# Reordered small work in a two-layer hybrid attention trunk: first squares, rotary roots, key copies, first output chunk

## The chip, the cores and the metric

The kernel runs on one core of one Trainium2 chip. The time is the device time of one execution in microseconds (us). Three runs of the kernel before gave a median of 1243.19 us (1242.96 to 1244.62). TensorE (PE) multiplies, VectorE (DVE), ScalarE (ACT) and GpSimd (POOL) do the elementwise work, and SyncE (SP) issues almost all transfers. Each engine works through its own queue in order.

## The reference

The trunk has two layers over two groups of tokens, 512 of a prompt and 256 of a sample, with 1024 channels. Each layer does, for each group:

```python
mod = silu(c) @ w_ada + b_ada                      # shift, scale, gate
hid = rms_norm(x, norm_g) * (1 + scale) + shift
qa, ka, va, za, qb, kb, vb, zb, ga, gb = split(hid @ w_in)
oa = neighbourhood_attention(qa, ka, va, rpb)      # 8 heads of 64, on a grid
ya = (oa * silu(za)) @ w_pa
ob = gqa(rope(rms_norm(qb)), rope(rms_norm(kb)), vb)   # 8 query heads, 2 key heads
yb = (ob * silu(zb)) @ w_pb
merged = sigmoid(ga) * ya + sigmoid(gb) * yb
x = x + gate * (merged @ w_out)
```

A last rms_norm ends the trunk. All arithmetic is float32.

## The kernel before

**Products.** Every matrix product is done in three passes on operands that are split into a high and a low part: high by high, low by high, high by low. The weights come from memory in units of 128 x 1024 (`raw`). ScalarE copies a unit to its high part (`whi`, line 222), and VectorE subtracts to get the low part (`wlo`, line 228); two or three units of a layer go to GpSimd instead. The helper `mm` at line 115 records every product, so that products are told apart by the tile they write: `accp` and `accs` are chunks of 256 output channels for the prompt and the sample, `accw` and `acct` have the tokens on the partitions.

**Stages of a layer.** The value projection of the neighbourhood branch (`va`), four head pairs of queries and keys with the neighbourhood attention beside them (`sp`, `tp`, `op`), the queries (`qb`) and the keys and values (`kvb`) of the grouped branch with norms and rotary positions, the gate `za`, then four pairs of chunks `ga`, `pa` with the grouped attention beside them (`gsp` scores, `gp` probabilities, `gtp` their transposes, `go` the product with the values), `zb`, four pairs `gb`, `pb` with the vectors of the next modulation computed on VectorE beside them (`adaacc`), and the output projection `wo`, first for the prompt and then for the sample.

**What sets the order.** The kernel's text is run once to write the program, under a manual schedule, so the order of its calls is the order in each engine's queue. The unit is a step: 6 to 12 products of one chunk, written by `step(fn)`. After each step the function writes what `defer(k, fn)` put off by k steps, then one piece of `chain` (the norm and the modulation of the next layer), then pieces of the attention from `slots` at a set rate, and pieces of `side` (`adaacc`). A table `SC` holds the offsets: the scaled keys come `KF` steps after the last step of `kvb`, their transposes `KT` steps after it, the grouped attention starts `SGQ` steps after it, the query roots and transposes of the prompt `QF` and `QT` steps after the queries' third pass, and `DP` steps after the prompt's output chunks the next norm starts. `ahead` splits the next chunk's weight units at two set steps of a chunk. In the 3 pieces of `rms_chain` the sum over channels is a product with ones (`ssps`), then come Newton steps for the inverse root on VectorE (`ny`, `na`, 11 small instructions), and then a product that spreads the roots (`rb`).

**The start.** The start of the program is planned: `job` records pieces with an engine, a duration and dependencies, `load` records transfers with times, and `run_jobs` writes all in order of the planned times. Squares of the 8 tiles of `x` are taken by ScalarE (`sq`) and added up by VectorE, two of them by GpSimd. The modulation vectors of the first layer are products on TensorE (`adap`) of 32 loaded pieces (`adaraw`), which come back through `rows` (ACT) and `adat` (PE). Products on zeroes (`junk`) keep TensorE running: 18 at first and then one for each 0.45 us of planned time.

**Grouped attention's entry.** `rope_finish` takes the roots of 32, 16 or 12 sums for each token and scales the rotated tiles (`rr`). `ktr` transposes the six key tiles (`kt`), and `evac_k` copies each to two places on ScalarE (`GK`, lines 675 and 676) and writes two low parts on VectorE (lines 679 and 680). The scores of the grouped attention rotate through two buffers: a third `gsp` needs the first one's row maximum (`gss`, line 902) and exponential (line 912) done.

## Time and profile before

| | |
|---|---|
| median of 3 runs | 1243.19 us |
| profiled execution, its own time | 1244.36 us |
| its span, first to last instruction | 1242.6 us |
| mean granted TensorE clock | 0.995 |
| PE busy | 1208.7 us (97%) |
| DVE busy | 818.4 us (66%) |
| ACT busy | 580.6 us (47%) |
| POOL busy | 347.6 us (28%) |

A row of a timeline gives the start, the duration, the engine, the line, what is written from what, and in square brackets how long the engine sat idle before it and what released it. A row of the waits gives who waited for whom: the sum in us, how often, and the longest. A row of the windows gives, for each stretch of the span, its length, the busy time of PE, PEld (weight loads), DVE, ACT and POOL with the number of instructions, the granted TensorE clock, the share of the DMA engines and GB/s.

### The profile page before, as it was taken

Reading aid. Unit: us, or ns where it says so; the run is one execution under the profiler, and the core shown is the slowest. Engines: PE = TensorE matmul, PEld = TensorE weight load, DVE = VectorE, ACT = ScalarE, POOL = GpSimd, SP = SyncE. Lnnn points to the kernel's source line nnn. Section 1 sums busy time; section 2 is a strip of 40 time slices with the busy share of each in tenths; the row PEclk is TensorE's granted clock in tenths of the full one; section 3 lists DMA queues with packets and bytes.
Section 4 is the critical chain, followed back from the end, with each engine's and each line's share of the span. In section 5 each row is a group of like instructions: output and inputs, shape, how many; then the busy total and the mean of one; then the engine's idle time right before and its main releaser. Section 6 shows DMA issues by size and latency. Waiting matters only on the chain.

```text
span 1242.6 us, 19501 instructions
## 1 busy us (share of the span) xinstructions
PE 1208.7 (97%) x7282; PEld 1058.6 (85%) x7282; DVE 818.4 (66%) x1609; ACT 580.6 (47%) x1229; POOL 347.6 (28%) x383
## 2 busy tenths in 40 slices
PE   8999999989999999999989999998999999999997
PEld 5789988879898988887888998897988998888887
DVE  5757877775556558998384688777566545683435
ACT  4447755445545332333153776554555543232323
POOL 0024555342223121121131443553322212121102
PEclk9999999999999999999999999999999999999999
DMA  9343411111011234556352324112011113332334
GB/s 350 138 124 94 108 54 54 49 51 35 26 44 51 69 107 149 170 169 202 119 172 88 93 74 124 35 38 65 18 52 52 35 35 102 119 105 66 119 102 152
DMA packets 48125, 118.28 MB, mean 95 GB/s; under 512 B 5408, under 2 KB 11936, under 8 KB 48032
## 3 DMA queue, kind: packets, MB, share of 16 engines
q1 hardware_dynamic: 47888, 116.98, 30.6%
q8 instruction: 57, 0.93, 0.3%
q14 instruction: 36, 0.29, 0.1%
q10 hardware_dynamic: 144, 0.07, 0.0%
HBM read 110.74 MB, written 6.29 MB: 94 GB/s over the span
## 4 chain that ended last, share of the span: by engine, by line
PE 78%; DVE 11%; ACT 5%; issue 3%; DMA 1%; POOL 1%; SPq 0%; DVEq 0%; ACTq 0%; POOLq 0%
PE accp L115 35%; PE accs L115 17%; PE accw L115 8%; PE go L115 3%; PE gsp L115 3%; PE gtp L937 3%; PE acct L115 3%; DVE adaacc L445 3%; DVE wlo L228 2%; ACT p L775 1%; PE sp L115 1%; PE op L115 1%; ACT whi L222 1%; PE adap L115 1%; DVE ptl L704 1%
## 5 line engine op out<-in xcount | busy, mean ns | idle before, releaser
L115 PE MATMUL accp<-hh,whi 128*128 128x512 f32 x512 | 204.3, 399 | 0.0
L115 PE MATMUL accp<-hh,wlo 128*128 128x512 f32 x512 | 201.2, 393 | 2.1 <-DVE wlo L228 2.1
L115 PE MATMUL accp<-hl,whi 128*128 128x512 f32 x512 | 201.2, 393 | 0.0
L228 DVE TENSOR_TENSOR wlo<-raw,whi 128x1024 fp32r<-128x1024 f32 x119 | 159.1, 1338 | 21.1 <-ACT whi L222 20.5
L115 PE MATMUL accs<-hh,whi 128*128 128x256 f32 x512 | 146.4, 286 | 0.0
L115 PE MATMUL accs<-hh,wlo 128*128 128x256 f32 x512 | 145.0, 283 | 0.0
L115 PE MATMUL accs<-hl,whi 128*128 128x256 f32 x512 | 144.9, 283 | 0.0
L926 POOL TENSOR_TENSOR gp<-gp,gss 128x512 f32<-128x512 f32 x80 | 83.4, 1042 | 213.8 <-DVE gss L924 192.5
L222 ACT ACTIVATE whi<-raw 128x1024 fp32r<-128x1024 f32 x124 | 129.7, 1053 | 17.7 <-PE accw L115 8.2
L115 PEld LDWEIGHTS accp<-hh,wlo 128*128 128x128 f32 x512 | 96.8, 189 | 24.9 <-DVE wlo L228 3.8
L115 PEld LDWEIGHTS accp<-hl,whi 128*128 128x128 f32 x512 | 97.1, 190 | 17.5
L115 PEld LDWEIGHTS accp<-hh,whi 128*128 128x128 f32 x512 | 96.8, 189 | 17.7
L699 ACT ACTIVATE pth<-gtp 128x512 fp32r<-128x512 f32 x80 | 47.7, 597 | 111.2 <-PE go L115 90.2
L115 PEld LDWEIGHTS accs<-hh,whi 128*128 128x128 f32 x512 | 98.2, 192 | 1.0
L115 PEld LDWEIGHTS accs<-hl,whi 128*128 128x128 f32 x512 | 98.2, 192 | 1.0
L115 PEld LDWEIGHTS accs<-hh,wlo 128*128 128x128 f32 x512 | 98.0, 191 | 0.0
L1539 POOL TENSOR_TENSOR th<-th 128x512 f32<-128x512 f32 (+1 forms) x32 | 43.5, 1371 | 171.2 <-DVE th L1532 171.2
L445 DVE SCALAR_TENSOR_TENSOR adaacc<-adaraw,csil,adaacc 128x512 f32<-128x512 f32 x112 | 86.6, 829 | 3.6 <-DMA adaraw<-in_wsd 3.6
L722 POOL TENSOR_TENSOR bm<-u,masks 128x128 f32<-128x128 f32 (+2 forms) x80 | 41.3, 539 | 152.4 <-DMA u<-in_rpb 152.4
L704 DVE TENSOR_TENSOR ptl<-gtp,pth 128x512 fp32r<-128x512 f32 x80 | 54.7, 685 | 40.5 <-ACT pth L699 40.4
L115 PE MATMUL accw<-whi,hh 128*128 128x512 f32 x192 | 77.3, 403 | 0.0
L115 PE MATMUL accw<-wlo,hh 128*128 128x512 f32 x192 | 75.3, 392 | 0.0
(245 smaller groups left out, 2965.7 us busy)
## 6 DMA issues: line engine op xcount, KB each, us to landing
raw<-in_wst SPq DMA_DIRECT2D x124, 512.0 KB, 3.6
adaraw<-in_wsd SPq DMA_DIRECT2D x64, 256.0 KB, 3.1
adaraw<-in_wad SPq DMA_DIRECT2D x32, 256.0 KB, 6.0
u<-in_rpb SPq DMA_DIRECT2D x16, 354.5 KB, 4.8
u<-in_rpb SPq DMA_DIRECT2D x16, 236.5 KB, 4.4
out_y<-y SPq DMA_DIRECT2D x12, 256.0 KB, 2.5
x<-in_xT SPq DMA_DIRECT2D x8, 256.0 KB, 5.0
res<-in_xT SPq DMA_DIRECT2D x8, 256.0 KB, 3.0
```

The costliest lines, as they stand in the source:

```text
L115: T.matmul(out=out, lhsT=lhsT, rhs=rhs, start=start, stop=stop, skip_group_check=True)
L222: A.activation(out=hi, in_=r, func=AF.Copy)
L228: eng.tensor_sub(out=lo, in0=r, in1=hi.bitcast(F32))
L445: V.scalar_tensor_tensor(out=acc[n, h, g], in0=r, scalar=c, in1=acc[n, h, g], op0=ALU.mult, op1=ALU.add)
L699: A.activation(out=h, in_=t, func=AF.Copy)
L704: V.tensor_sub(out=lo, in0=t, in1=h.bitcast(F32))
L722: G.tensor_tensor(out=o.rearrange("p (c r) -> p c r", r=r), in0=u, in1=mk.rearrange("p (c r) -> p c r", r=r), op=ALU.add)
L775: A.activation(out=P[:, j, :], in_=P[:, j, :], func=AF.Exp, scale=-1.0, bias=ss[:, j:j + 1], accum_out=ss[:, 2 + j:3 + j])
L926: G.tensor_mul(out=pv_, in0=pv_, in1=ss[:, 4:4 + n].unsqueeze(2).to_broadcast([128, n, w]))
L937: T.transpose(t[:, q, 128 * j:128 * j + 128], src, ident)
L1539: G.tensor_add(out=t[:, sl], in0=t[:, sl], in1=mrg[k][:, sl])
```

## The change

**The start.** All adding of squares goes to VectorE, in order of the tiles, for tiles 0 to 6; tile 7's squares are summed by a product of their own, into the same accumulator. The products on zeroes are 30 at once, and then one for each gap of over 0.5 us that the plan leaves on TensorE up to 20 us. The planned transfers move by 0.7 us and the plan's delay between engines goes from 0.12 to 0.22 us.

**Norms.** An empty piece stands between the Newton steps and the spreading product, and `DP` is 5 in place of 6. For the sample's norm of the second layer there is one empty piece more.

**Rotary roots.** The Newton steps are written in two halves one step apart, and the scalings one step each after them. The offsets move: `QF` 5 to 4, `QT` 9 to 10, `QS` 6 to 5, `QST` 12 to 13, `KF` 7 to 5.

**Keys.** The transposes and copies are done for the prompt at step 12 (before: all at 13) and for the sample at 14, and the second key head's copies follow one step after the first's. The grouped attention starts at step 15 in place of 16.

**Weights and the first output chunk.** In chunks four tiles deep (`pa`, `pb`) the next units are split at steps 2 and 4 in place of 3 and 6, and in the sample's output chunks at 1 and 2 in place of 2 and 3. In the first output chunk the products with the last two merged tiles are put behind all others of that chunk.

```diff
-    T0=3.6,
+    T0=4.3,
-    WARM=(18, 18.0, 0.45),
+    WARM=(30, 20.0),
-    QF=5,  QT=9,  QS=6,  QST=12,  KF=7,  KT=13,  SGQ=16,  DP=6,
+    QF=4,  QT=10, QS=5,  QST=13,  KF=5,  KT=12,  SGQ=15,  DP=5,
...
     def paired(pieces):
-        return pieces[0:3] + [sum(pieces[i:i + 2], []) for i in range(3, len(pieces), 2)]
+        return pieces[0:4] + [sum(pieces[i:i + 2], []) for i in range(4, len(pieces), 2)]
...
-    def newton(x, n):
+    def newton_parts(x, n):
+
         y = smp.tile([128, n], F32, tag=f"ny{n}", name="ny", bufs=1)
         a = smp.tile([128, n], F32, tag=f"na{n}", name="na", bufs=1)
...
+        return y, [first, refine, refine, refine]
+
+    def newton(x, n):
+        y, parts = newton_parts(x, n)
+        for fn in parts:
+            fn()
         return y
...
-        return [[a_], [b_], [c_]]
+        return [[a_], [b_], [], [c_]]
...
-    def feat_chunk(name, src, nk, evac, ksteps=2, groups=(0, 1), keep=False, sep=False):
+    def feat_chunk(name, src, nk, evac, ksteps=2, groups=(0, 1), keep=False, sep=False, late=False):
...
+            kk = per * (1 + g)
+            seq = [(m, k0) for m in range(2) for k0 in range(0, nk, kk)]
+            if late:
+                seq = [p for p in seq if p[1] < nk - kk] + [p for p in seq if p[1] == nk - kk]
+            for m, k0 in seq:
...
-                        if not (keep and name[2] == 3) and cnt[0] in ((3, 6) if len(groups) == 2 else (3, 5) if groups[0] == 0 else (2, 3)):
+                        if not (keep and name[2] == 3) and cnt[0] in ((2, 4) if nk == 4 else (3, 6) if len(groups) == 2 else (3, 5) if groups[0] == 0 else (1, 2)):
                             ahead(name)
...
-        def run_jobs(lag=0.12):
+        def run_jobs(lag=0.22):
...
+            n0, until = SC["WARM"]
+            t = 1.8 + 0.3 * n0
+            for j in sorted((j for j in jobs if j["eng"] == "PE"), key=lambda j: done[j["n"]]):
+                start = done[j["n"]] - j["dur"]
+                while t + 0.5 < min(start, until):
+                    out.append((t, -1, lambda: warm(1)))
+                    t += 0.3
+                t = max(t, done[j["n"]])
+            warm(n0)
...
-        def sq_sum():
-            hcell["ps"] = ps_acc.tile([128, 4], F32, tag="acc", name="ssps")
+        def sq_sum(k, first, last):
+            if first:
+                hcell["ps"] = ps_acc.tile([128, 4], F32, tag="acc", name="ssps")
             for i in range(4):
-                mm(hcell["ps"][:, i:i + 1], sq[0, 0][:, 128 * i:128 * i + 128], ones[:, 0:1], i == 0, i == 3)
-            gfree(sq.pop((0, 0)))
+                mm(hcell["ps"][:, i:i + 1], sq[0, k][:, 128 * i:128 * i + 128], ones[:, 0:1],
+                   first and i == 0, last and i == 3)
+            gfree(sq.pop((0, k)))
...
-        jg = job("POOL", 1.2, [js[2], js[3]], lambda: sq_add(0, 3, 2, G), 1)
-        j = js[0]
-        for k, d in ((1, js[1]), (4, js[4]), (2, jg), (5, js[5]), (6, js[6]), (7, js[7])):
-            j = job("DVE", 0.75, [j, d], lambda k=k: sq_add(0, k, 0, V), 1)
-        j = job("PE", 0.95, [j], sq_sum, 0)
-        jsum = [j]
+        ja = js[0]
+        for k in range(1, KC - 1):
+            ja = job("DVE", 0.85, [ja, js[k]], lambda k=k: sq_add(0, k, 0, V), 1)
+        jsum = [job("PE", 0.95, [js[-1]], lambda: sq_sum(KC - 1, True, False), 0)]
+        jsum.append(job("PE", 0.95, [ja, jsum[0]], lambda: sq_sum(0, False, True), 0))
...
-        plan.append((-100, -1, lambda: warm(W0)))
-        t = SC["T0"] + 2
-        while t < WE:
-            plan.append((t, -1, lambda: warm(1)))
-            t += WS
...
             def rope_finish(rs, ss):
-                V.tensor_scalar(out=ss, in0=ss, scalar1=1.0 / 64, scalar2=EPS, op0=ALU.mult, op1=ALU.add)
-                y = newton(ss.rearrange("p t h -> p (t h)"), n * nh).rearrange("p (t h) -> p t h", h=nh)
+                y, parts = newton_parts(ss.rearrange("p t h -> p (t h)"), n * nh)
+                yv = y.rearrange("p (t h) -> p t h", h=nh)
+                def roots():
+                    V.tensor_scalar(out=ss, in0=ss, scalar1=1.0 / 64, scalar2=EPS, op0=ALU.mult, op1=ALU.add)
+                    parts[0]()
+                    parts[1]()
+                def roots2():
+                    parts[2]()
+                    parts[3]()
+                roots()
+                defer(1, roots2)
                 t = 0
                 for i, r in enumerate(rs):
                     k = r.shape[1]
-                    t += k
-                    if i < 2:
-                        scale()
-                    else:
-                        defer(i // 2, scale)
+                    defer(2 + i, lambda r=r, k=k, t=t: V.tensor_mul(
+                        out=r, in0=r, in1=yv[:, t:t + k, :].unsqueeze(3).to_broadcast([128, k, nh, 64])))
+                    t += k
...
-            def ktr():
+            def ktr(g):
...
+                evac_k(GK[0][0], GK[0][1], 0, t, slice(c, c + n))
+                defer(1, lambda: evac_k(GK[1][0], GK[1][1], 1, t, slice(c, c + n)))
...
-            defer(SC["KT"], ktr)
+            defer(SC["KT"], lambda: ktr(0))
+            defer(SC["KT"] + 2, lambda: ktr(1))
...
                 feat_chunk(("wo", l, i), merged, KC, lambda m, g, ps, i=i: wev(m, g, ps, i), groups=(0,),
-                           keep=i >= 2)
+                           keep=i >= 2, late=i == 0)
...
-                chain.extend([[], []] + paired(hid_chain(l + 1, 1, xn)))
+                rest = paired(hid_chain(l + 1, 1, xn))
+                chain.extend([[], []] + rest[:2] + [[]] + rest[2:])
```

The offsets of `SC` are put on two lines here. The changed file is 29 lines longer, so a line number of the changed kernel is a little higher than that of the same work before (line 680 is 693).

**VectorE's queue where the grouped attention starts in layer 0**, before:

```order
L1454 TENSOR_TENSOR zl<-zt,zh 128x512
L1440 SCALAR_TENSOR_TENSOR zt<-zt,accp 128x512
L1454 TENSOR_TENSOR zl<-zt,zh 128x512
L679 TENSOR_TENSOR GK<-kt,GK 64x512
L680 TENSOR_TENSOR GK<-kt,GK 64x512
L679 TENSOR_TENSOR GK<-kt,GK 64x512
L680 TENSOR_TENSOR GK<-kt,GK 64x512
L679 TENSOR_TENSOR GK<-kt,GK 64x256
L680 TENSOR_TENSOR GK<-kt,GK 64x256
L679 TENSOR_TENSOR GK<-kt,GK 64x256
L680 TENSOR_TENSOR GK<-kt,GK 64x256
L1440 SCALAR_TENSOR_TENSOR zt<-zt,accs 128x256 x2
```

And in the changed kernel:

```order
L1482 TENSOR_TENSOR zl<-zt,zh 128x512
L1468 SCALAR_TENSOR_TENSOR zt<-zt,accp 128x512
L692 TENSOR_TENSOR GK<-kt,GK 64x512
L693 TENSOR_TENSOR GK<-kt,GK 64x512
L1482 TENSOR_TENSOR zl<-zt,zh 128x512
L1468 SCALAR_TENSOR_TENSOR zt<-zt,accs 128x256 x2
L692 TENSOR_TENSOR GK<-kt,GK 64x512
L693 TENSOR_TENSOR GK<-kt,GK 64x512
L692 TENSOR_TENSOR GK<-kt,GK 64x256
L693 TENSOR_TENSOR GK<-kt,GK 64x256
L228 TENSOR_TENSOR wlo<-raw,whi 128x1024
L692 TENSOR_TENSOR GK<-kt,GK 64x256
```

The first key head's two low parts for the prompt now stand ahead of the second `zl`, and a split of weights stands among the copies for the sample.

**VectorE's queue at the roots of the prompt's queries in layer 0** (`ptl` is the low part of the transposed probabilities that the neighbourhood attention's `op` reads), before:

```order
L365 SCALAR_TENSOR_TENSOR ny<-na,ny 128x32
L1333 TENSOR_TENSOR rr<-rr,ny 128x512 x2
L704 TENSOR_TENSOR ptl<-tp,pth 128x512
L1333 TENSOR_TENSOR rr<-rr,ny 128x512 x2
L1308 TENSOR_REDUCE qss<-rsq 128x8 x2
```

And in the changed kernel:

```order
L369 SCALAR_TENSOR_TENSOR ny<-na,ny 128x32
L717 TENSOR_TENSOR ptl<-tp,pth 128x512
L1363 TENSOR_TENSOR rr<-rr,ny 128x512 x3
L1327 TENSOR_REDUCE qss<-rsq 128x8
L1363 TENSOR_TENSOR rr<-rr,ny 128x512
L1327 TENSOR_REDUCE qss<-rsq 128x8
```

All four scalings now stand behind the second `ptl`; the first `ptl` stands between the two halves of the roots.

**TensorE's queue at the start**, before:

```order
L115 MATMUL junk<-cst 128x512 x29
L115 MATMUL adap<-adaraw,c_104 32x256 x4
L115 MATMUL junk<-cst 128x512 x3
L115 MATMUL adap<-adaraw,c_104 32x256 x4
L115 MATMUL junk<-cst 128x512 x2
L115 MATMUL ssps<-ones,sq 128x1 x4
L115 MATMUL junk<-cst 128x512 x2
L115 MATMUL adat<-sel,rows 128x2 x2
```

And in the changed kernel:

```order
L115 MATMUL junk<-cst 128x512 x30
L115 MATMUL ssps<-ones,sq 128x1 x4
L115 MATMUL adap<-adaraw,c_104 32x256 x8
L115 MATMUL ssps<-ones,sq 128x1 x4
L115 MATMUL adat<-sel,rows 128x2 x2
L115 MATMUL adap<-adaraw,c_104 32x256 x8
L115 MATMUL junk<-cst 128x512 x2
L115 MATMUL rb<-ident,ny 128x128 x4
```

Two products on zeroes are left between the first 30 and the value projection, where 17 stood; one more group of four `ssps` stands there.

More of the change, by code (lines that the diff above doesn't have):

```diff
@@ L37 @@
     RQ=31,
-    QF=5,
-    QT=9,
+    QF=4,
+    QT=10,
     QTT=2,
-    QS=6,
-    QST=12,
-    KF=7,
-    KT=13,
-    SGQ=16,
+    QS=5,
+    QST=13,
+    KF=5,
+    KT=12,
+    SGQ=15,
     RG=84,
@@ L52 @@
     TL=3,
-    DP=6,
+    DP=5,
     DPE=4,
@@ L583, in feat_chunk @@
         for g in groups:
-            for m in range(2):
-                kk = per * (1 + g)
-                for k0 in range(0, nk, kk):
+            kk = per * (1 + g)
[3 more added lines that the diff above has]
+            for m, k0 in seq:
                     def f(g=g, m=m, k0=k0, kk=kk):
@@ L1195, in sample_sum @@
             sums[0][0]()
-        sums = rms_chain(1, scell)
+        sums = [p for p in rms_chain(1, scell) if p]
         j = job("PE", 0.4, jadd + [jfin[0, 3], jfin[1, 3], jva[-6]], sample_sum, 0)
```

36 lines of the change are left out of this document (17 added, 19 removed).

## The prediction

> **What bounds the kernel now.** I read the page's busy times first, then the waits of TensorE, then windows and timelines of the places where it waits.
>
> ```profile
> span 1242.6 us, 19501 instructions
> PE 1208.7 (97%) x7282; PEld 1058.6 (85%) x7282; DVE 818.4 (66%) x1609; ACT 580.6 (47%) x1229; POOL 347.6 (28%) x383
> ```
>
> TensorE is the bound: 33.9 us of the span are not busy. The change takes no product of the model away, so it can win only what TensorE waits, what it loses at a lower clock, and filler at the start. The waits:
>
> ```profile
> PE gsp L115 <- ACT gp L912: 5.6, 2, 3.6
> PE op L115 <- DVE ptl L704: 5.2, 4, 1.6
> PE gsp L115 <- DVE GK L680: 4.1, 2, 2.0
> PE rb L115 <- DVE ny L365: 3.1, 2, 1.7
> PE accp L115 <- DVE wlo L228: 2.7, 5, 1.0
> ...
> PE accp L115 <- DVE ml L1563: 1.3, 1, 1.3
> ```
>
> The largest two, 9.7 us, stand where the grouped attention starts, once in each layer. Windows there show a second price, the granted clock (the column behind the five busy times):
>
> ```profile
> 253.70:257.12 3.42, 0.52 (x2) 0.47 (x3) 2.97 (x5) 2.52 (x5) 1.57 (x2) 1.00 0.54 153
> 257.12:260.53 3.41, 3.41 (x11) 2.75 (x11) 2.56 (x6) 1.75 (x4) 1.73 (x2) 0.50 0.40 101
> ...
> 851.04:854.45 3.41, 1.38 (x7) 0.84 (x6) 2.19 (x4) 2.73 (x6) 0.00 (x0) 1.00 0.00 0
> 854.45:857.87 3.42, 3.42 (x9) 2.65 (x9) 3.32 (x8) 0.00 (x0) 0.00 (x0) 0.50 0.03 5
> ...
> 861.28:864.69 3.41, 1.77 (x8) 1.47 (x9) 3.15 (x4) 1.59 (x3) 1.40 (x2) 1.00 0.31 124
> ```
>
> After 3.4 us with 0.52 or 1.38 us of products the clock is half for the next 3.4 us. That loses 1.7 us in each layer, 3.4 us in all. A window with 1.77 us of products was followed by none.
>
> **The change part by part.** *Grouped attention's entry.* In layer 0:
>
> ```profile
> 240.74 0.82 PE L1418 MATMUL kt<-ident,rr 128*128 128x128 f32 x6
> ...
> 241.38 0.59 ACT L675 ACTIVATE GK<-kt 64x512 fp32r<-64x512 f32 x1 [4.54 <-PE kt L1418]
> ...
> 245.26 0.62 ACT L1450 ACTIVATE zh<-zt 128x512 fp32r<-128x512 f32 x1
> ...
> 247.21 0.68 DVE L680 TENSOR_TENSOR GK<-kt,GK 64x512 fp32r<-64x512 f32 x1
> ...
> 247.94 0.50 PE L115 MATMUL gsp<-GK,GQ 128*128 128x512 f32 x1 [2.03 <-DVE GK L680]
> ...
> 253.34 0.68 DVE L902 TENSOR_REDUCE gss<-gsp 128x1 f32<-128x512 f32 x1
> ...
> 255.78 0.68 ACT L912 ACTIVATE gp<-gsp,gss 128x512 f32<-128x512 f32 x1
> ...
> 256.60 0.80 PE L115 MATMUL gsp<-GK,GQ 128*128 128x512 f32 x2 [3.60 <-ACT gp L912]
> ```
>
> VectorE's low parts of the keys stand behind a `zl` whose `zh` stands on ScalarE behind eight key copies (3.9 us). Now only two copies (1.2 us) and two low parts (1.4 us) lie between the transposes and the first `gsp`, and both stand ahead of that pair. The transposes come one step earlier; with the some 1.2 us that the parts below win before this place I put them at 238.1, the copies end by 240.0, the low parts by 240.8, and the first `gsp` follows three steps and both transposes later, at 243.1. Its wait goes: -4.1 us in two layers. What queues next is late: the other key copies, `zh` and `whi` on ScalarE, then the low parts, `wlo` and the first `gss`. From the durations above ScalarE ends its copies at 245.8, VectorE `wlo` at 246.6 and the last low parts at 247.5, `gss` ends at 248.2, and `gp`, ready behind the `zt` of the next chunk, at 249.1. TensorE gets to the third `gsp` at 248.2 and so waits 0.9 us. I leave 1.0 us in each layer of 5.6: -3.6 us. A wait of 1 us leaves enough products in a window, so both half clocks go: -3.4 us. Bounds: nothing of the 5.6 and 3.4 goes, or all does. The cover is thin at one point: the scaled keys leave VectorE at about 237.7, 0.4 us before their transposes, since `wlo` now stands ahead of them.
>
> *Roots of the queries.*
>
> ```profile
> 199.17 1.29 DVE L1333 TENSOR_TENSOR rr<-rr,ny 128x512 f32<-128x512 f32 x2
> ...
> 200.38 0.68 DVE L704 TENSOR_TENSOR ptl<-tp,pth 128x512 fp32r<-128x512 f32 x1
> ...
> 201.12 0.39 PE L115 MATMUL op<-ptl,v 128*128 128x256 f32 x1 [1.61 <-DVE ptl L704]
> ```
>
> The second `ptl` waits for all roots and two scalings. Without the scalings ahead it comes 1.21 us earlier, 1.2 of the 1.6 us, twice: -2.4 us (0 to -3.2). The other two `op` waits, 1.0 us each, lie in the neighbourhood attention before these roots and stay. All four scalings move behind that `ptl`, the last to one step ahead of the queries' transposes, which themselves go one step later; a step's 1.36 us (below) against 0.64 us for one scaling leaves the transposes their cover.
>
> *Norms.* One step of 12 sample products more between `ny` and `rb` is 1.44 us, since one begins 0.12 us after another (619.69 and 619.81 below); two steps of the second layer's `va` are 2.7 us. Against waits of 1.4 and 1.7 us this leaves 0.1: -3.0 us (-3.1 to -1.5). The sum `ssps` moves a step ahead at the first; its adds ended at 614.1, some four steps before the products at 619.69 that stand behind it:
>
> ```profile
> 613.42 0.68 DVE L347 TENSOR_TENSOR ssq<-ssq,sq 128x512 f32<-128x512 f32 x1
> ...
> 619.69 0.28 PE L115 MATMUL accs<-mv,wlo 128*128 128x256 f32 x1
> 619.81 0.40 PE L115 MATMUL accs<-mv,whi 128*128 128x256 f32 x2
> ```
>
> *Weights and first output chunk.* `wlo` is written at least a step (6 products of the prompt, 0.227 us from one to the next in the rows below: 1.36 us) earlier, against five waits of at most 1.0; the products on the last `ml` come three steps, 4.1 us, later, against 1.3. But VectorE has little room where four of these five waits lie:
>
> ```profile
> 500.75 0.39 PE L115 MATMUL accp<-zh,whi 128*128 128x512 f32 x1
> 500.98 0.39 PE L115 MATMUL accp<-zl,whi 128*128 128x512 f32 x1
> ...
> 470.00:570.00 100.00, 97.06 (x537) 80.94 (x537) 95.46 (x133) 33.54 (x54) 22.35 (x16) 1.00 0.54 166
> ```
>
> Of 2.7 + 1.3 us I take 3.5 (0 to -4.0).
>
> *The start.*
>
> ```profile
> 6.88 3.98 ACT L1145 ACTIVATE sq<-x 128x512 f32<-128x512 f32 x6 [0.92 <-DMA x<-in_xT]
> 8.87 4.41 DVE L1148 TENSOR_TENSOR sq<-sq 128x512 f32<-128x512 f32 x5 [2.19 <-ACT sq L1145]
> 11.60 5.71 SPq L1082 DMA_DIRECT2D adaraw<-in_wad  x8
> ...
> 14.22 0.95 PE L115 MATMUL ssps<-ones,sq 128*128 128x1 f32 x8
> ...
> 18.95 1.05 PE L115 MATMUL rb<-ident,ny 128*128 128x128 f32 x8
> ...
> 24.84 0.50 PE L115 MATMUL accw<-whi,hh 128*128 128x512 f32 x1
> ...
> adaraw<-in_wad SPq DMA_DIRECT2D x32, 256.0 KB, 6.0
> ```
>
> The squares end at 10.9 and the adds at 13.3; adds in order end near 12, so that the last `ssps` begin near 13 in place of 14.22, behind two groups of `adap`. GpSimd's add leaves a path where it cost nothing. The first `accw` needs 32 `adap`, as before; the 16th load is issued by 17.3, when the row of eight issues ends, and lands a median of 6.0 us after an earlier issue, at some 22.4. With the 1.2 us of the earlier `ssps`, `rb` would end at 18.8 in place of 20.0, near 17.5 without the fillers between, and the loads decide: the first `accw` can start near 22.7 in place of 24.84. Later loads land at a fixed pace and hold it back at the second and third group, so I take -1.8 us (+1.6 to -2.2: with one half-clock window 1.7 us go back, and one more for an uncovered wait).
>
> *The end.* The prompt's last output piece comes one step later, still ahead of the last sample tile: 0.
>
> New places for `whi` and `wlo` between scores of the grouped attention, and VectorE's shifts of queue, cost something that no row shows: between 0 and 5 us, I take +2.0, since 262 to 470 us shows no wait of TensorE in the list above and VectorE is free there for 91 of 208 us:
>
> ```profile
> 262.00:470.00 208.00, 208.00 (x1309) 186.86 (x1308) 116.80 (x206) 97.98 (x210) 52.24 (x49) 1.00 0.18 55
> ```
>
> **Sum.** -4.1 - 3.6 - 3.4 - 2.4 - 3.0 - 3.5 - 1.8 + 2.0 = -19.8 us, from the profiled execution's 1244.4 to 1224.6. That execution lies 1.2 us above the median of the runs, so the forecast is 1223.4 us.
>
> The Trainium skill, in "TensorE: Matmul & The Clock Gate", section "Why this matters for your kernels", warns of idle gaps above about 3 us only. By that rule the gap of 2.0 us in layer 1 would cost no clock and 1.7 us less would be won, 1225.1; this case's window at 851.04, with 1.38 us busy, was followed by a half clock, so the trace speaks for the larger gain.
>
> **The rivals.** *The exponential still comes late:* VectorE's queue at the entry has no less in it, only another order, so the third `gsp` waits 3.6 us once and 2.0 once as now, with both half clocks: 3.6 and 3.4 us go back, 1230.4. For it: VectorE's 2.97 of 3.42 us at 253.7. Against: `zl` and `zt` of the sample now stand ahead of the copies they held up. *A cold start:* with few fillers, TensorE's clock is half when `accw` begins; up to 3.4 us go back, 1226.8. For it: the two `adap` groups ahead are short products; against: if the loads set the first groups, slower products there end no later. *The keys are not ready:* `wlo` of 1.34 us (the group's mean below) or more ahead of the scaling makes the transposes wait, and the 4.1 us stay: 1227.5. That is the change not doing what it says. *Slower:* the splits moved in `pa` fall between a score and its exponential. 16 units are moved there in two layers, each 1.05 us on ScalarE and 1.34 on VectorE:
>
> ```profile
> L228 DVE TENSOR_TENSOR wlo<-raw,whi 128x1024 fp32r<-128x1024 f32 x119 | 159.1, 1338 | 21.1 <-ACT whi L222 20.5
> ...
> L222 ACT ACTIVATE whi<-raw 128x1024 fp32r<-128x1024 f32 x124 | 129.7, 1053 | 17.7 <-PE accw L115 8.2
> ```
>
> If TensorE waits for both, 2.4 us each, nine of the 16 eat the gain, and twelve (28.7 us) give 1252. Against it: both engines are free half of that stage.
>
> **How the numbers follow.** The forecast has 0.58, with its own range of 1218 to 1229; the late exponential 0.16, the cold start 0.11, the late keys 0.08, the slower case 0.07. The range takes in the first three rivals and, below, all bounds of the waits but the start's: 1216 to 1233. What this kernel's timing can tell from no change is about 0.2%, 2.5 us. Faster by more has 0.91: the first four cases, with 0.02 of them lost to sums of mishaps; within it 0.03, slower 0.06, since a part of the last case only eats the gain.
>
> **What would show it.** Right: no wait of `gsp` on `GK`, waits of `gsp` on `gp` of about 1 us, no half clock near 257 and 854, `op` waits near 0.4 after the roots, none on `ny`, the first `accw` near 22.7. Wrong: `kt` waiting for `rr`, many short waits of `gsp` between 262 and 470, a granted clock of 0.5 in the first 30 us, or a wait of `qt` for `rr`.

## The result

The changed kernel took 1225.58 us (median of four runs, 1225.34 to 1225.68) against 1243.9 us for the kernel before on the same chip: a ratio of 0.985, with a 95% interval of 0.983 to 0.987. The forecast was 1223.4 us. The profiled execution took 1225.67 us over a span of 1223.9 us. The page's busy times, after:

```profile
span 1223.9 us, 19495 instructions
PE 1202.9 (98%) x7276; PEld 1056.5 (86%) x7276; DVE 816.6 (67%) x1609; ACT 579.7 (47%) x1229; POOL 342.9 (28%) x382
```

The waits of TensorE, after (who waited for whom, us in total, how often, the longest):

```profile
PE kt L1444 <- DVE rr L1363: 3.1, 2, 1.6
PE gsp L115 <- ACT gp L925: 2.6, 2, 1.3
PE ssps L115 <- ACT sq L1168: 2.1, 1, 2.1
PE op L115 <- DVE ptl L717: 2.0, 2, 1.0
...
PE rb L115 <- DVE ny L369: 0.6, 2, 0.4
```

The waits on `GK`, on `wlo` of the prompt and on `ml` are gone, two of the four on `ptl` too, and `rb` keeps 0.6 of 3.1 us. One is new: the key transposes `kt` wait for the scaled keys `rr`, 1.5 us in each layer, which was named beforehand as a sign of error. Three of the scarcest windows of the middle of the span, with the granted clock behind the five busy times (a fourth, at 830.64, held 2.02 us of products):

```profile
236.72:240.13 3.41, 1.86 (x14) 1.60 (x14) 3.41 (x5) 1.38 (x3) 1.79 (x1) 1.00 0.47 131
246.96:250.37 3.41, 2.23 (x10) 1.50 (x8) 3.30 (x7) 2.51 (x8) 0.00 (x0) 1.00 0.36 94
840.88:844.29 3.41, 2.09 (x10) 1.42 (x9) 3.33 (x8) 2.46 (x5) 0.27 (x1) 1.00 0.54 154
```

None falls to 1.4 us of products, as two windows did before, and the clock stays at 1.00 up to the last 7.5 us.

**Where the time went, stage by stage.** Every kernel of this study issues the same 5472 products with weights (`accp`, `accs`, `accw`, `acct`) in nearly the same order, so the time from the n-th to the m-th can be compared across kernels. The table gives it in us from one profiled execution each, by the starts of the products, which are counted from 0: from the start to product 450, then from 450 to 880 and so on; "last" runs from product 4436 to the end of the span. Products 880 to 1700 and 3616 to 4436 hold the entry of the grouped attention in the two layers. A few transposes and small products lie on the other side of a boundary when they move by a step.

| kernel | to 450 | to 880 | to 1700 | to 2600 | to 2900 | to 3616 | to 4436 | last |
|---|---|---|---|---|---|---|---|---|
| before | 136.0 | 99.51 | 205.80 | 175.34 | 59.91 | 165.25 | 204.26 | 196.5 |
| changed | 135.3 | 98.34 | 201.32 | 170.72 | 56.91 | 163.88 | 201.33 | 196.1 |
| changed, again | 136.6 | 98.32 | 201.32 | 170.72 | 57.06 | 163.90 | 201.30 | 196.4 |
| keys alone | 136.1 | 99.58 | 202.85 | 175.29 | 60.03 | 165.14 | 201.25 | 196.7 |
| query roots alone | 136.1 | 98.30 | 204.26 | 175.31 | 59.95 | 164.02 | 204.27 | 197.2 |
| the rest alone | 135.5 | 99.52 | 204.25 | 170.74 | 56.93 | 165.14 | 204.26 | 196.1 |
| before with filler | 136.4 | 99.53 | 205.83 | 175.29 | 60.09 | 165.25 | 204.30 | 196.7 |
| first `zt` product on VectorE | 135.2 | 98.32 | 204.55 | 170.74 | 56.93 | 163.90 | 203.25 | 195.9 |
| key scalings early | 134.9 | 98.32 | 202.31 | 170.74 | 58.01 | 163.90 | 203.91 | 196.3 |
| attention at step 16 | 136.5 | 98.33 | 199.93 | 170.75 | 57.08 | 163.91 | 200.01 | 196.1 |
| step 16 and tables spread | 134.8 | 96.95 | 200.01 | 170.74 | 57.89 | 162.54 | 200.03 | 196.2 |
| four edits, step 16 | 135.2 | 96.95 | 199.75 | 170.72 | 57.07 | 162.53 | 199.76 | 196.1 |
| four edits, step 17 | 134.7 | 96.94 | 199.83 | 170.74 | 57.50 | 162.51 | 199.77 | 195.9 |
| five edits | 135.5 | 96.95 | 198.01 | 170.98 | 57.32 | 162.52 | 198.01 | 195.9 |

Most cells repeat within 0.1 us in kernels that agree in that stage. The start scatters by 1.9 us, "last" by 0.5 to 0.7, and "to 2900" by up to 1.1: in three kernels a product (`accw`) waits there 0.3 to 0.7 us for `xn`, and what brings that wait was not looked into. From before to changed the columns give -0.7, -1.17, -4.48, -4.62, -3.00, -1.37, -2.93 and -0.4, which is the 18.7 us of the span.

### The profile page after: what moved, and what is told of

Its sections match the earlier page's. It is cut to its first block, busy times and chain, and to the rows that moved or that the text cites. A ratio compares the mean times of both kernels' runs of the same rounds, so it can differ in the third digit from the quotient of the medians.

```text
span 1223.9 us, 19495 instructions
## 1 busy us (share of the span) xinstructions
PE 1202.9 (98%) x7276; PEld 1056.5 (86%) x7276; DVE 816.6 (67%) x1609; ACT 579.7 (47%) x1229; POOL 342.9 (28%) x382
## 4 chain that ended last, share of the span: by engine, by line
PE 81%; DVE 10%; ACT 4%; issue 2%; DMA 2%; POOL 0%; SPq 0%; DVEq 0%; ACTq 0%; POOLq 0%
PE accp L115 37%; PE accs L115 19%; PE accw L115 9%; PE go L115 3%; PE gsp L115 3%; PE gtp L950 3%; PE acct L115 2%; DVE wlo L228 2%; ACT p L788 1%; PE sp L115 1%; DVE GQ L681 1%; DMA adaraw<-in_wad 1%; PE op L115 1%; PE adat L115 1%; DVE ptl L717 1%
## 5 line engine op out<-in xcount | busy, mean ns | idle before, releaser
L915 DVE TENSOR_REDUCE gss<-gsp 128x1 f32<-128x512 f32 x64 | 43.8, 685 | 51.9 <-PE gsp L115 51.6
```

The lines of the kernel that those rows point to most:

```text
L915: V.tensor_reduce(out=ss[:, 0:1], in_=sp, axis=AX.X, op=ALU.max, negate=True)
```

## The experiments

Each of four sets was timed together with the kernel before on one chip; ratios are to that. Times of different sets are compared by ratios only.

**1. The keys alone.** The kernel before, with `ktr` of the change and three offsets; the roots keep their one piece:

```diff
-    KF=7,
-    KT=13,
-    SGQ=16,
+    KF=5,
+    KT=12,
+    SGQ=15,
...
-            defer(SC["KT"], ktr)
+            defer(SC["KT"], lambda: ktr(0))
+            defer(SC["KT"] + 2, lambda: ktr(1))
```

> The kernel before with the key part alone: transposes and copies in pieces, KF 5, KT 12, SGQ 15; the Newton steps of the roots stay in one piece and the scalings follow them at once, and everything else is as before. Theory A (the new wait of kt on rr, 1.71 us in each layer of the changed kernel, comes from the halved roots, which put the key scalings two steps later on VectorE): no wait of kt above 0.5 us, the waits of gsp on GK gone (-4.4), those of gsp on gp down to about 1.5 each (-3.0), both half-clock windows gone (-2.7): -10.1, 1233.8 us. Theory B (VectorE is simply late there, whatever the order): kt waits 1.7 us in each layer here too, -6.7, 1237.2 us. Theory C (the exponential still comes late): gsp on gp waits 3.6 and 2.0 as before and the half clocks stay, -4, 1240 us.

Measured: 0.994 (0.9925 to 0.9956), 1238.6 us, so 6.7 us less than the 1245.28 of the kernel before in this set. `kt` did not wait, so its wait in the changed kernel does come with the halved roots. But the third `gsp` waited 2.3 us in each layer in place of 1.3:

```profile
PE gsp L115 <- ACT gp L912: 4.6, 2, 2.3
```

The stage of the second layer took 201.25 us, with the changed kernel's 201.33. The two are equal by chance: the transposes come 1.7 us earlier than in the changed kernel, the third score 0.74 us earlier (the table behind experiment 12), and 400 products into the stage the keys alone are still 0.77 us ahead. Then a product of the grouped attention (`go`) waits 0.42 us for `ob`, once in each layer, and 0.7 us are lost again. So of the wait on `kt` less than half was to be won at the entry. Theory A was right on the cause and wrong on the price.

**2. The query roots alone.** The kernel before with the new `rope_finish` for the queries and their four offsets (QF 4, QT 10, QS 5, QST 13).

> The kernel before with the query roots alone: halves, scalings one step apart, QF 4, QT 10, QS 5, QST 13; the keys keep the old finish. Theory A: both second waits of op on ptl (1.77 us of lost spacing each) go whole, the waits at the key entry stay as before: -3.5, 1240.4 us. Theory B (the prediction's term): 0.4 us of each stays, -2.4, 1241.5 us. Theory C: the queries' scalings are late for their transposes, a wait of qt on rr takes the gain, 1243.9 us.

Measured: 0.997 (0.9956 to 0.9979), 1241.3 us. The second waits of `op` on `ptl` are gone from the list (2.0 us in two waits are left of 5.2 in four), and yet the stages with them win 1.21 and 1.23 us (99.51 to 98.30, 165.25 to 164.02): 2.4 in all, less than the waits' 1.6 each. The rest stands in the timeline, in idle times of some 0.1 us that are too short for the list:

```profile
199.37 0.28 PE L115 MATMUL op<-pth,v 128*128 128x256 f32 x1
199.74 0.38 PE L115 MATMUL op<-ptl,v 128*128 128x256 f32 x1
...
215.48 0.28 PE L115 MATMUL acct<-whi,hl 128*128 128x256 f32 x1
215.86 0.63 PE L1401 MATMUL qt<-ident,rr 128*128 128x128 f32 x4
```

These products start 0.12 us apart where nothing waits. The `op` on `ptl` still starts 0.37 us after the product ahead of it, and the last transposes of the queries (`qt`), which now come a step later, 0.38 us: 0.25 us are lost at each. Theory A describes the list of waits, theory B the gain.

**3. The rest alone.** The changed kernel with `rope_finish`, `ktr` and the seven offsets as before.

> The changed kernel with the roots, the keys and their seven offsets put back: the start, the norms, the weights and the first output chunk alone. Theory A (the parts add up): start -0.7, norms -2.9, waits on wlo and ml -4.9 and some 0.5 of small ones: -9.0, 1234.9 us. Theory B (the prediction's terms): start -1.8, norms -3.0, weights -3.5, -8.3, 1235.6 us. Theory C (what the entry wins is given back later, so that these places win more or less in its company): these places differ from the changed kernel's by more than 1 us.

Measured: 0.992 (0.9901 to 0.9931), 1235.34 us. The stages "to 2600" and "to 2900" win the same 4.6 and 3.0 us as in the whole change: 170.74 against 170.72, 56.93 against 56.91. By the medians the three parts give -0.6, -0.3 and -0.8%, in all -1.7 or -1.8%, against -1.5% of the whole. At one place the overlap can be seen: the roots and the rest, which change nothing at the entry itself, each win 1.5 us in "to 1700" of layer 0 (204.26 and 204.25 in place of 205.80), and the whole wins it once. Experiment 4 shows what it is.

**4. Filler in the waits of the kernel before.** Fourteen products on zeroes in each layer, where TensorE waits at the entry:

```diff
+            if h == 0 and i == 2:
+                fill(8)
...
                 mm(sp, q, Kh[:, 0:NP], True, False)
+                if h == 0 and i == 0:
+                    fill(6)
                 mm(sp, q, Kl[:, 0:NP], False, True)
```

> The kernel before with 14 products on zeroes in each layer where TensorE waits at the entry: 6 of them between the first score's two products, 8 ahead of the third score, into a buffer that nothing else uses then. Some 1.4 and 1.8 us of filler lie inside waits of 2.2 and 2.2 to 3.8 us. Theory A (a 3.4 us window with too few products is followed by a half clock): both half-clock windows go, the waits end where they ended, -2.7, 1241.2 us. Theory B (only a gap of over 3 us brings the half clock): the one in layer 0, behind 3.8 us, goes, the one in layer 1, behind 2.2 us, stays: -1.4, 1242.5 us. Theory C (the half clock has another cause, or the filler costs what it saves): both stay or nothing is won, 1243.9 us or more.

Measured: 1.000 (0.9992 to 1.001). All three theories had it otherwise in part: the half clock of layer 1 is gone, that of layer 0 is still there, and neither stage moved (205.83 and 204.30). Windows of this kernel:

```profile
254.81:258.22 3.41, 1.64 (x7) 1.03 (x6) 3.01 (x3) 2.15 (x5) 1.26 (x1) 1.00 0.52 153
258.22:261.63 3.41, 3.41 (x14) 3.04 (x14) 2.56 (x6) 2.44 (x6) 2.08 (x2) 0.50 0.54 150
862.38:865.79 3.41, 2.31 (x12) 1.97 (x13) 2.99 (x4) 1.18 (x4) 1.94 (x2) 1.00 0.22 89
```

1.64 us of products were not enough. In the keys alone one wait of 2.3 us was followed by a half clock in layer 0 and not in layer 1:

```profile
249.19:252.61 3.42, 1.10 (x5) 0.67 (x4) 3.31 (x9) 2.53 (x6) 0.10 (x1) 1.00 0.47 153
252.61:256.02 3.41, 3.41 (x9) 2.67 (x8) 2.69 (x4) 1.59 (x6) 3.41 (x3) 0.50 0.12 26
...
853.35:856.77 3.42, 1.63 (x7) 1.37 (x8) 3.36 (x8) 2.23 (x5) 0.95 (x1) 1.00 0.52 153
856.77:860.18 3.41, 3.41 (x22) 3.02 (x21) 2.56 (x6) 1.92 (x6) 3.41 (x4) 1.00 0.35 74
```

The windows lie on a fixed grid (in the kernel before, the one half clock ends at 260.53 and the other starts at 854.45, 174 windows of 3.413 us later), and where a wait falls on it differs from one execution to the next. Over all fourteen profiles, from 30 us on and up to the last 20 us, every window at full clock with 1.46 us of products or less was followed by a half clock, none with 1.70 or more was, and 1.63 and 1.64 went one each way. Busy time alone does not settle it: a window that was itself at half clock had 2.75 us of products and was followed by another (experiment 5), and among the short products of the start and the end, windows with up to 2.5 us were followed by a half clock.

What a half clock costs depends on where it falls. In layer 1 it stood in the kernel before, in the roots alone and in the rest alone, and not with filler, and the stage took 204.26, 204.27, 204.26 and 204.30 us: there the slow products lie ahead of a score that has to wait anyway. In layer 0 it stood behind the third score in the kernel before and with filler (205.80, 205.83), and ahead of it in the roots alone, whose windows show it:

```profile
244.31:247.73 3.42, 1.38 (x7) 0.82 (x6) 2.85 (x5) 2.08 (x4) 0.00 (x0) 1.00 0.00 0
247.73:251.14 3.41, 3.41 (x10) 2.63 (x9) 3.33 (x8) 0.00 (x0) 0.63 (x1) 0.50 0.00 0
```

There and in the rest alone the stage took 1.5 us less. So a half clock taken away alone was worth 1.5 us in layer 0 of that one execution, and nothing in layer 1, where the wait behind it lasts 2.0 us in place of 3.6. Two later pairs agree: behind the third score a half clock cost 1.60 us in the keys alone (202.85 against 201.25) and 1.60 in the key scalings early (203.91 against 202.31).

**5. What holds up the scaled keys.** The timeline of the changed kernel at the key scalings (start, duration, engine, line, operation):

```profile
236.16 1.22 DVE L228 TENSOR_TENSOR wlo<-raw,whi 128x1024 fp32r<-128x1024 f32 x1
236.32 2.18 POOL L1471 TENSOR_TENSOR zt<-zt,oa 128x512 f32<-128x512 f32 x1 [4.86 <-DVE zt L1468]
237.30 2.09 DVE L1363 TENSOR_TENSOR rr<-rr,ny 128x512 f32<-128x512 f32 x2
239.20 0.63 PE L1444 MATMUL kt<-ident,rr 128*128 128x128 f32 x4 [1.55 <-DVE rr L1363]
```

The two scalings take 2.09 us, the first of them 1.76. GpSimd's product ends at 238.50, and that first scaling 0.56 us later. The experiment moves that product to VectorE, behind the scalings:

```diff
-                for d, fn in ((1, z1), (2, z2), (4, z3), (5, z4)):
+                first = o is oa and chunk == 0 and m == 0 and g == 0
+
+                def z2v():
+                    V.tensor_mul(out=z[:, sl], in0=z[:, sl], in1=o[k][:, sl])
+
+                for d, fn in ((1, z1), (3, z2v) if first else (2, z2), (4, z3), (5, z4)):
```

> The changed kernel with one product of gate and attention output in each layer (the first prompt tile of za, which GpSimd computes in 2.18 us while VectorE's key scaling takes 1.76 us) moved to VectorE, one step later, behind the key scalings. Theory A (VectorE's scaling waits until GpSimd's instruction ends): the scaling takes 0.7 us, kt waits 0.6 to 0.7 in place of 1.7 us in each layer; since VectorE has 0.7 us more to do, the third gsp gets a part of it back: -2.1 to 0, 1223.5 to 1225.6 us. Theory B (the scaling takes 1.76 us for its own reasons, its operands or their place): it still takes 1.7 us, kt waits as long as before, 1225.6 us or more.

Measured: the same two scalings take 1.02 us, and `kt` waits 0.46 us here:

```profile
237.16 1.02 DVE L1363 TENSOR_TENSOR rr<-rr,ny 128x512 f32<-128x512 f32 x2
...
237.99 0.63 PE L1444 MATMUL kt<-ident,rr 128*128 128x128 f32 x4 [0.46 <-DVE rr L1363]
```

So VectorE's scaling waited until GpSimd's instruction was done. The Trainium skill says so in "SBUF — State Buffer", section "🔬 SBUF: two separate sides": VectorE and GpSimd share a pair of ports, which a GpSimd instruction that reads SBUF, or a VectorE instruction with two inputs in SBUF, holds for its whole length while the other is blocked. The trace agrees: 1.76 us beside GpSimd, 0.69 without. Theory A is right on the cause. But the kernel became slower, which it had excluded: 0.988 (0.9864 to 0.9893), 1230.56 us: the third score now waited 2.8 us in place of 1.3, and each of the two waits brought a half clock, the first for two windows:

```profile
250.09:253.50 3.41, 2.75 (x7) 2.17 (x8) 3.41 (x7) 2.34 (x5) 2.06 (x2) 0.50 0.30 119
253.50:256.92 3.42, 3.42 (x10) 2.65 (x9) 0.88 (x4) 1.29 (x3) 3.19 (x3) 0.50 0.53 153
```

The score itself started only 0.35 us later than in the changed kernel (the table behind experiment 12), so the half clocks are most of the loss.

**6. The key scalings early.** The scalings right behind the second half of their roots, ahead of `zt` and `wlo` on VectorE:

```diff
-                    defer(2 + i, lambda r=r, k=k, t=t: V.tensor_mul(
+                    defer(1 if nh == 2 else 2 + i, lambda r=r, k=k, t=t: V.tensor_mul(
```

> The changed kernel with the two key scalings written right behind the second half of their roots, ahead of a zt and a wlo in VectorE's queue, in both layers. Theory A (the order alone makes kt wait, and the third gsp waits for its own reason): no wait of kt, gsp on gp stays at 1.5 each: -3.4, 1222.2 us. Theory B (VectorE is behind with its work here, and a wait removed comes back at the next product that needs it, as the keys alone had 2.5 us on gp and none on kt): no wait of kt, but gsp on gp, or on the keys, grows to 2.5 or more in all: -1.4 to 0, 1224.2 to 1225.6 us.

Measured: 0.988 (0.986 to 0.990), 1230.3 us, slower than the changed kernel; both theories had it no slower. The wait of `kt` is gone, and the two behind it are longer by more than that:

```profile
PE gsp L115 <- ACT gp L925: 6.2, 2, 3.1
...
PE gsp L115 <- DVE GK L693: 1.3, 2, 0.7
```

One wait of 3.1 us falls more easily below the limit of a window than two of 1.5 and 1.3: here it did in layer 1 (203.91 against 202.31 in layer 0, where it did not). Layer 0 lost 1.0 us even so, and the timeline shows to what:

```profile
236.80 1.22 DVE L228 TENSOR_TENSOR wlo<-raw,whi 128x1024 fp32r<-128x1024 f32 x1
236.96 2.21 POOL L1471 TENSOR_TENSOR zt<-zt,oa 128x512 f32<-128x512 f32 x1 [5.99 <-DVE zt L1468]
239.20 0.63 ACT L1478 ACTIVATE zh<-zt 128x512 fp32r<-128x512 f32 x1 [7.65 <-POOL zt L1471]
239.87 0.69 DVE L1482 TENSOR_TENSOR zl<-zt,zh 128x512 fp32r<-128x512 f32 x1 [1.85 <-ACT zh L1478]
```

The scalings now stand ahead of VectorE's first `zt`, which starts GpSimd's product, and with it `zh` and `zl`. VectorE idles 1.85 us for `zh`, and all that stands behind `zl` comes 1.0 us later. The wait on `kt` was no loss to be won back in this way. It stood ahead of a longer one.

**7. The attention one step later.** SGQ 16 in place of 15, nothing else.

> The changed kernel with the grouped attention one step later (SGQ 16 in place of 15), nothing else. Theory A (the third gsp waits for VectorE's backlog, which does not hang on when the first scores come): kt keeps its 1.7 us, gsp on gp falls from 1.5 to about 0.1 in each layer: -2.7, 1222.9 us. Theory B (the row maximum and the exponential simply follow the scores a step later): gsp on gp stays at 1.5, 1225.6 us.

Measured: 0.983 (0.9811 to 0.9841), 1223.53 us. `kt` waits as before and `gsp` not at all; the stages lose 1.39 and 1.32 us (201.32 to 199.93, 201.33 to 200.01), as theory A has it. With a step of 1.36 us of products ahead of it, the third score comes when its buffer is free.

**8. Four edits at once.** To SGQ 16 and the early scalings come the first za tile's `zh` and `zl` two steps later and the four products of the rotary tables (`tab`), which stood ahead of the low part that the first `op` waits for, one step apart:

```diff
-                    V.tensor_mul(out=tb[:, :, s, :], in0=tr[:, :, s, :],
-                                 in1=gn[:, 2 * w + s].unsqueeze(1).to_broadcast([128, 6, 64]))
+                    defer(4 + 2 * w + s, lambda s=s, w=w, tb=tb: V.tensor_mul(
+                        out=tb[:, :, s, :], in0=tr[:, :, s, :],
+                        in1=gn[:, 2 * w + s].unsqueeze(1).to_broadcast([128, 6, 64])))
...
-                for d, fn in ((1, z1), (2, z2), (4, z3), (5, z4)):
-                    defer(d, fn)
+                e = 2 if o is oa and chunk == 0 and m == 0 and g == 0 else 0
+                for d, fn in ((1, z1), (2, z2), (4 + e, z3), (5 + e, z4)):
+                    defer(d, fn)
```

> The changed kernel with four edits: the key scalings right behind their roots, the grouped attention at step 16, the high and low part of the first za tile two steps later, and the four products of the rotary tables spread over four steps, since they stand ahead of the low part that the first op waits for. Theory A (VectorE has room behind each of these places): kt -3.4, gsp on gp -2.9, op on ptl -2.3: -8.6, 1217.0 us. Theory B (the backlog at the entry comes back as waits of gsp): only op goes and about 2 us of the rest: -4.3, 1221.3 us. Theory C (the tables are late for the products that need them, or the attention, begun later, is not done when zb begins): 1225.6 us or more.

Measured: 0.980 (0.9786 to 0.9819), 1220.58 us. The waits of `op` are gone (98.33 to 96.95, 163.91 to 162.53: 1.38 us a layer against step 16 alone), that of `kt` too, and the third score waits 1.4 us again. The gain over the changed kernel is 2.7 us in `op` and 3.1 at the two entries (201.32 to 199.75, 201.33 to 199.76), between the two theories: a part of the backlog came back, as B says, but less of it.

**9. The same without the early scalings** and without the later `zh` and `zl`: SGQ 16 and the spread tables alone.

> The changed kernel with the grouped attention at step 16 and the rotary tables spread, while the key scalings and the first za tile stay where the change put them. Theory A (the third score is ready at a time that VectorE's and ScalarE's queues set, so that the key scalings' place is worth nothing as long as the scores come no later): kt waits 1.7 us, gsp on gp nothing, op nothing: as fast as the version that also moved the scalings, 0.980 of the kernel before. Theory B (each wait is worth its length): 0.1 us per layer apart from that version too, but for the opposite reason, so the profile decides: under A the third gsp comes as long after the last product of kvb's steps in both.

Measured: 0.980 (0.979 to 0.9819), 1221.03 us, with 1.5 us of wait on `kt` in each layer and none on `gp`; the entry stages take 200.01 and 200.03 us against 199.75 and 199.76. The place of the scalings, together with that of the first za tile's `zh` and `zl`, is worth 0.3 us a layer, not the 1.5 of the wait. What each of the two is worth beside the other was not measured. Theory A.

**10. One step more.** The four edits with SGQ 17 and the rate over 83 steps.

> The version with four edits, with the grouped attention at step 17 in place of 16 (and the rate of its pieces over 83 steps in place of 84). Theory A (one step, 1.4 us, more before the scores takes up the 1.6 us that the third gsp waits): gsp on gp falls to about 0.2 in each layer, -2.8 against step 16, 0.978 of the kernel before, some 9 us faster than the changed kernel. Theory B (the exponential follows the scores): still 1.6 us, 0.980. Theory C (attention that begins later ends too late and holds up zb): slower than step 16.

Measured: 0.980 (0.9783 to 0.9814), 1219.72 us, no different from step 16. The third score still waits 1.48 us. The row maximum (`gss`), which comes a step after the scores, now has two `zl` and a `zt` ahead of it on VectorE and starts 1.4 us later, counted from product 880, than at step 16:

```profile
246.66 0.76 DVE L1483 TENSOR_TENSOR zl<-zt,zh 128x256 fp32r<-128x256 f32 x2
247.45 0.69 DVE L1469 SCALAR_TENSOR_TENSOR zt<-zt,accp 128x512 f32<-128x512 f32 x1
248.06 0.68 DVE L915 TENSOR_REDUCE gss<-gsp 128x1 f32<-128x512 f32 x1
...
249.61 0.73 PE L115 MATMUL gsp<-GK,GQ 128*128 128x512 f32 x2 [1.48 <-ACT gp L925]
```

**11. The changed kernel again**, beside 9 and 10.

> The changed kernel itself once more, on the chip of the two kernels below: 0.985 of the kernel before. If the waits at the entry are split in two of 1.7 and 1.5 us in each layer as in its first profile, no window before the end is followed by a half clock; at the start the loads of x have no hole this time, or have one again, which shifts the first accw by about 1 us.

Measured: 0.985 (0.9834 to 0.9864), 1226.34 us (1225.29 to 1227.47). From product 450 on, the stages repeat within 0.2 us up to product 4436, and no half clock falls in them; the start differs by 1.3 us. ScalarE waited 0.65 us for a late load of `x` this time, in place of 1.46.

**12. Less work ahead of the row maximum.** If queues set when the third score starts, work has to leave them. The second key head is read only by the fifth to eighth query head; its copies move behind the first row maximum, on top of the four edits at step 16:

```diff
-                defer(1, lambda: evac_k(GK[1][0], GK[1][1], 1, t, slice(c, c + n)))
+                defer(7 - g, lambda: evac_k(GK[1][0], GK[1][1], 1, t, slice(c, c + n)))
```

> The version with four edits (grouped attention at step 16) with one more: the second key head's copies, whose four low parts take 2.3 us of VectorE and whose high parts 2.0 us of ScalarE, five to six steps later, behind the first row maximum and exponential. That head is read only by the fifth to eighth query head. Theory A (the queues of VectorE and ScalarE set when the third score can start): the first row maximum comes some 2 us earlier, the 1.6 us on gp go in each layer, -3.2, 0.978 of the kernel before. Theory B (the scores and the exponential set it themselves, or the copies now stand in the way of the next exponentials): the third or the fifth score still waits as much, 0.980.

Measured: 0.977 (0.9759 to 0.9786), 1217.01 us, the fastest of the study and some 9 to 10 us below the changed kernel by the ratios. VectorE and the scores with four edits, and then with five:

```profile
246.24 0.43 DVE L692 TENSOR_TENSOR GK<-kt,GK 64x256 fp32r<-64x256 f32 x1
246.68 0.43 DVE L693 TENSOR_TENSOR GK<-kt,GK 64x256 fp32r<-64x256 f32 x1
247.13 0.69 DVE L915 TENSOR_REDUCE gss<-gsp 128x1 f32<-128x512 f32 x1
247.86 0.69 ACT L925 ACTIVATE gp<-gsp,gss 128x512 f32<-128x512 f32 x1
...
248.69 0.74 PE L115 MATMUL gsp<-GK,GQ 128*128 128x512 f32 x2 [1.44 <-ACT gp L925]
```

```profile
243.80 1.48 DVE L228 TENSOR_TENSOR wlo<-raw,whi 128x1024 fp32r<-128x1024 f32 x1
245.20 0.68 DVE L915 TENSOR_REDUCE gss<-gsp 128x1 f32<-128x512 f32 x1
...
245.98 0.68 ACT L925 ACTIVATE gp<-gsp,gss 128x512 f32<-128x512 f32 x1
```

Counted from product 880, the row maximum starts 2.3 us earlier and the exponential follows. No wait of `gsp` is left in either layer, and the stages lose 1.74 and 1.75 us. Theory A.

**What sets the third score.** The starts at the entry of the second layer, in us from product 3616 (layer 0 gives the same within 0.03):

| kernel | first `zt` on VectorE | first `kt` | first row maximum | third score |
|---|---|---|---|---|
| changed | 1.91 | 5.55 | 15.30 | 16.86 |
| keys alone | 1.24 | 3.84 | 14.55 | 16.11 |
| first `zt` product on VectorE | 1.87 | 4.44 | 15.64 | 17.20 |
| key scalings early | 3.02 | 3.84 | 16.31 | 17.87 |
| attention at step 16 | 1.87 | 5.52 | 15.26 | 16.82 |
| four edits, step 16 | 3.02 | 3.84 | 15.02 | 16.58 |
| four edits, step 17 | 3.00 | 3.84 | 16.41 | 17.96 |
| five edits | 3.03 | 3.84 | 12.74 | 14.99 |

Except with five edits, the third score starts 1.55 to 1.56 us after the first row maximum, whenever `kt` starts. And in the changed kernel, the keys alone, the scalings early and step 16 the maximum starts 13.3 to 13.4 us after the first `zt`, whether the scalings stand behind that `zt` or ahead of it: where they stand ahead, VectorE idles 1.85 us for `zh` in their place. So the entry is a chain that begins with this `zt`, and it is shortened by beginning it earlier or by taking work out of it.

## Why the prediction was right

The total came out 2.2 us above the forecast: 1.1 us by the sum of the terms, and the rest because the profiled execution of before lay 1.2 us above its median and that of the changed kernel on its own. The errors of the terms reach 3.7 us and have both signs, so that the total came this close is partly luck. By its terms, measured on the profiled executions:

- **Grouped attention's entry**, -4.1 - 3.6 - 3.4 = -11.1 forecast. Measured: -4.48 in layer 0 and -2.93 in layer 1, in all -7.4. The rows add up to this. In each layer the wait on `GK` went whole, 2.03 us, the half clock gave back 1.7, and the new wait on `kt` takes 1.55; the wait on `gp` went from 3.60 and 2.04 to 1.3. That is -2.03 - 1.7 - 2.29 + 1.55 = -4.5 in layer 0 and -2.03 - 1.7 - 0.71 + 1.55 = -2.9 in layer 1. So "both half clocks go: -3.4 us" held as a term of this sum, though a half clock taken away alone gives nothing in layer 1 (experiment 4). What failed is "its wait goes: -4.1 us": the scaled keys were to be ready "0.4 us before their transposes", and they came 1.6 us late, 1.1 us of it behind GpSimd's product. That costs 3.1 us in two layers, to which the forecast gave nothing but a warning that the cover was thin. The third `gsp` waited 1.3 us in each layer, where 1.0 was left: 0.6 us. The rival "the keys are not ready" was right about the wait, and 3.1 of its 4.1 us came. Taking that wait away gives back less than its length, since the third score hangs on another chain (experiments 1, 6 and 9).
- **Roots of the queries**, -2.4. Measured -2.4 in experiment 2, and -2.5 in the whole change (98.34, 163.88). Of the wait of 1.6 us all but 0.1 went, against 1.2 in the forecast, but only 1.2 reached the stage: the rest of that wait and a new one of 0.1 us at the last `qt` lose 0.25 us each (experiment 2).
- **Norms**, -3.0. Measured -3.0, with 0.6 us of wait left on `ny` in place of 0.1: 0.4 at the sample's norm of the second layer and 0.2 at a later one.
- **Weights and first output chunk**, -3.5. Measured -4.6 up to product 2600, and about 0.9 more between products 4436 and 5300, where one of the five waits lay: -5.6. All six waits went, where 3.5 of their 4.0 us were forecast to go, and each was worth more than its row says. A row of the waits counts the idle time only. The kernel before at the wait between products 4436 and 5300:

```profile
1086.15 0.39 PE L115 MATMUL accp<-hl,whi 128*128 128x512 f32 x1
1087.58 0.50 PE L115 MATMUL accp<-hh,wlo 128*128 128x512 f32 x1 [1.04 <-DVE wlo L228]
1087.92 0.40 PE L115 MATMUL accp<-hh,whi 128*128 128x512 f32 x1
```

The idle time is 1.04 us. But such products last 0.39 us and start 0.23 us apart where nothing waits; here 1.43 and then 0.34 us lie between the starts, so that 1.3 us are lost. The six waits of 4.0 us in the list lost 5.6 us in this way. One new wait, of `adat` for `adalo`, takes 0.4 us back, and small ones win 0.3. VectorE was busy for 98.7 of the 100 us from 470 to 570 and kept every wait away there:

```profile
470.00:570.00 100.00, 100.00 (x554) 85.13 (x553) 98.68 (x141) 32.97 (x55) 19.72 (x15) 1.00 0.56 172
262.00:470.00 208.00, 208.00 (x1289) 185.99 (x1289) 117.00 (x203) 96.90 (x205) 49.52 (x46) 1.00 0.19 58
```

- **New places for `whi` and `wlo`**, +2.0. Measured 0: TensorE is busy for all of 262 to 470 us (above). The new wait of `adat`, 0.4 us, lies elsewhere and is counted above.
- **The start**, -1.8. Measured -0.7 at product 450. Over all executions the ten with the new start pass it at a median of 135.3 us, the four with the old one at 136.1: -0.9. "The 16th load ... lands ... at some 22.4" is the step that failed: it landed at 23.3 in the changed kernel, and between 22.2 and 23.9 with the new start, against 22.2 to 22.4 with the old. The first `accw` started 0.6 us after it, at 23.94 and not near 22.7. In the first profile SyncE issued that load at 18.03, 1.0 us later than before; in the second it issued it at 17.02, as before, and it landed at 23.9. Why was not tested. In the first profile ScalarE also waited 1.46 us for a load of `x`, behind which the first `ssps` waited 2.1 us; in the second these were 0.65 and 0.6 us, and it was no faster at product 450.
- **The end**, 0. Measured about +0.5 behind product 5300, within what that stretch scatters.

The sum of these is -7.4 - 2.5 - 3.0 - 5.6 + 0 - 0.7 + 0.5 = -18.7 us. The forecast overrated the entry by 3.7 us and the start by 1.1, and underrated the weights by 2.1, with 2.0 us for new waits that did not come.

The late exponential, the rival held likeliest, did not stay (3.6 and 2.0 us became 1.3 each). Its reason, that the queue has no less in it, is what bounded the entry: taking work out of the queue (experiment 12) brought the third score forward by 1.6 us, starting the queue's work earlier (experiment 1) by 0.74, and experiment 7 put products into the wait. The cold start did not come in the changed kernel, in whose first 30 us no window was at half clock. But it can come with this start, which the attention at step 16 has too: there a late load left TensorE waiting 1.08 us, and the first `accw` ran at half clock:

```profile
19.56:22.98 3.42, 2.20 (x18) 0.98 (x16) 2.56 (x6) 1.60 (x3) 0.00 (x0) 1.00 1.04 391
22.98:26.39 3.41, 3.41 (x13) 2.01 (x10) 1.65 (x3) 1.33 (x2) 0.00 (x0) 0.50 1.05 389
```

It is one of the ten executions with the new start, and one of the two slowest at product 450 (136.5 us). The slower case did not come: no score waited for its exponential between 262 and 470 us.

## What to carry to other kernels

A wait is worth its length only if nothing waits behind it: where the next product needs the end of a long queue on another engine, removing a wait ahead of it makes the last one longer, by a part of its length or by more, so look for what ends the stage, and take work out of that queue. Where nothing waits behind it, a wait costs more than its idle time, here some 0.27 us more. Compare kernels by the time between the same two products of the bound engine rather than by lists of waits; these stage times repeated to 0.1 us where the medians of the kernel before differed by 2 us from set to set. But two equal stage times can hide a gain and a loss, as in experiment 1, so cut the stage finer before reading them as equal. Before trusting a planned lead of some tenths of a microsecond on VectorE, look whether GpSimd works at that time.

## What was not expected of the hardware

In the middle of the span, the limit of products in a window of 3.41 us at full clock below which the next runs at half clock lies near 1.6 us: 1.46 us and less always brought it, 1.70 and more never, and 1.63 and 1.64 went one each way. It is no limit for every window: one at half clock with 2.75 us brought it, and so did 2.20 us among the short products of the start. Since the windows start at a place that differs between executions, the same wait of 2.3 us cost a half clock in one layer and not in the other. And a VectorE instruction of 0.69 us took 1.76 us beside a GpSimd instruction that had started before it.
